# A two-layer hybrid encoder in split fp32: order of matmuls in both linear routines, one PSUM bank for the layer norm's two sums, and the loads and stores at both ends

## The chip, the cores and the metric

The kernel runs on one core of a Trainium2 chip, in one launch. The metric is the device time of that launch in microseconds (us); lower is better. The engines are TensorE (PE in the profile, with its weight loads as PEld), VectorE (DVE), ScalarE (ACT), GpSimd (POOL) and SyncE (SP), which issues most of the DMAs. Each engine works through its own instructions in the order in which they were put there.

## The reference

Two encoder layers on 256 tokens of width 2048, all in float32, with 256 memory tokens:

- layer 0's mixer: RMS norm, then one input projection. Part of its columns go through a gated depthwise convolution of width 31, a layer norm over 1024 channels and a swish; the other part is differential attention with 8 heads. Both results side by side go through one output projection.
- layer 1's mixer: RMS norm, an S5 state-space layer, gelu and a gated projection.
- in both layers, then: cross-attention (4 heads) into the memory tokens, and a gated feed-forward part with a convolution of width 3 and 5632 hidden channels.
- a last RMS norm.

```python
def layer_norm(x, g, b, eps=LN_EPS):
    mu = jnp.mean(xf, axis=-1, keepdims=True)
    var = jnp.mean(jnp.square(xf - mu), axis=-1, keepdims=True)
    y = (xf - mu) * lax.rsqrt(var + eps) * g.astype(jnp.float32) + b.astype(jnp.float32)
...
def mixer_conv_diff(xn, w_in, ...):
    z = xn @ w_in
    a_out = conformer_conv(a_val, a_gate, conv_dw, conv_db, conv_ln_g, conv_ln_b)
    b_out = diff_attention(...)
    return jnp.concatenate([a_out, b_out], axis=-1) @ w_out
```

## The kernel before, in words

**Weights and numbers.** Nearly all of the work is products of activations with large weight matrices. To keep float32 accuracy each operand is split into a high part, rounded to fp32r, and the low rest: a product is high times high, high times low and low times high. `wtile` (L200 to L213) brings in one weight tile of 128x1024 numbers (512 KB): a DMA on SP's queue into `raw` (four buffers, shared with the attention's `kvraw`), a cast on ACT into `hi`, a subtraction on DVE into `lo` (three buffers each).

**lin_ws** (L237 to L256) holds weights stationary. For each of the 16 slices of 128 input channels (kk within a tile, four tiles) and each of two column halves c it issues two matmuls: `both` (L250, weights `hi`, moving the 512 columns [high x, low x]) and a low one (L253, weights `lo`, moving the 256 columns of high x). Both accumulate in the PSUM bank of c: the low one in that bank's half for index 1, since `ps[:, c, 1]` collects all corrections. Low and high alternate, except at the very start of a call. Its users are the input projection (without its value columns), the memory keys, the queries and the feed-forward's up projection.

**lin_xs** (L263 to L291) holds x stationary and moves 512 weight columns: three matmuls (high-high, high-low, low-high) for token block tb = 0 into one bank, then three for tb = 1 into the other. With `tail=3` the last three weight tiles' matmuls for tb = 1 are issued after all those of tb = 0 (L290), which only the very last call uses.

**What sets the order.** Instructions of all engines are put in order by a scheduler that works on the program with a model of times. Side work (the convolution and layer norm `conv_ln`, the S5 parameters) are generators that `background` (L215) advances by a few DVE operations per weight tile, against a credit.

**PSUM.** `pst` (L73) gives single banks under two tags, "ps" and "pt", two buffers each, in turn if no tag is named. The differential attention's heads take "ps" for their scores and "pt" three times each (`ps_wT`, `ps_o`, `ps_oT`). A bank is reused when the reader of the tile that had it two requests earlier under that tag is done. The heads stand ahead of the memory keys and values (`mem_kv`) in the program, and the layer norm's end is played during those, so its two banks `ps_mu` (L516) and `ps_var` (L525) are requested after those of all heads. From `ps_var` come the variance and the reciprocal root on DVE (L528, then `rsqrt_steps`, L109), a multiplication (L532), swish on ACT (L537) and the split into `ao` (L299, L300). `ao` is the second half of the output projection's input (L494 to L500; its first half is the attention's `bo`).

**Start and end.** `setup` (L79) loads the first quarter of x, the identity matrix and the gains on SP, and `mixer0` loads five small tables on POOL's queue (L355 to L363). `xt_first` (L190) loads the other quarters between the first weight tiles, and `transpose_chunk` (L146) transposes them on PE. At the end (L692 to L709) the last quarter of x gets its product added, both token blocks' sums of squares are finished, a Newton iteration gives the reciprocal roots, ACT and DVE scale x, and eight DMAs store it.

## Time and profile before

| | |
|---|---|
| median of 3 runs | 2935.66 us (2931.55 to 2938.13) |
| the profiled execution | 2932.71 us, its span 2930.9 us |
| busy: PE / DVE / ACT / POOL | 98% / 76% / 51% / 9% of the span |
| matmuls | 16769, as many weight loads |
| DMA | 674 MB, 230 GB/s on average |
| granted TensorE clock | 0.994 on average |

The profile is of one execution. Times in its rows count from the first instruction; "[2.35 <-DMA raw]" says that the engine had stood idle for 2.35 us and what ended that. A matmul's own duration holds its way through the array, so two successive matmuls overlap: what one costs in a stream is read from the difference of starts. In rows with "x2" two equal instructions in succession are merged, and the time given is from the first's start to the last's end.

### The profile page before, as it was taken

The page shows a single profiled execution, that of the slowest core. Times are in us where ns is not written, and L with a number is a line of the kernel's source. Part 1 is how long each engine was busy: PE and PEld are TensorE (multiplying, and loading weights), DVE is VectorE, ACT ScalarE, POOL GpSimd, SP SyncE. Part 2 cuts the span into 40 slices and gives each one's busy share as a digit, 9 for nine tenths or more (in the row PEclk, how much of TensorE's full clock was granted, in tenths as well). Part 3 has the DMA queues.
Part 4 walks back from the last instruction along what each step waited for, and adds up shares of the span by engine and source line. Part 5 has one row for each costly group of instructions (what it writes and reads, how often), then busy time and mean ns, then how long its engine had stood idle before and what let it go on. Part 6 is the DMA issues. An engine that isn't in the chain of part 4 may idle for free. (4 is left out here: it accounts for less than half of the span.)

```text
span 2930.9 us, 44468 instructions
## 1 busy us (share of the span) xinstructions
PE 2881.2 (98%) x16769; PEld 2436.5 (83%) x16769; DVE 2213.4 (76%) x3568; ACT 1493.2 (51%) x2015; POOL 268.2 (9%) x509
## 2 busy tenths in 40 slices
PE   8999998999999999999999999999999999999998
PEld 7887887788888888888887787888888888888886
DVE  7899987877899987889855894656567776467764
ACT  5545554554455543455544554545455554345543
POOL 2100022222210012020021121000000000000000
PEclk9999999999999999999999999999999999999999
DMA  6655578988997687776697787655455555555554
GB/s 220 231 188 172 190 238 270 297 260 277 292 297 250 233 272 256 266 254 234 235 316 275 288 328 276 208 187 187 161 191 191 186 188 192 194 189 184 190 188 150
DMA packets 206023, 674.16 MB, mean 230 GB/s; under 512 B 33152, under 2 KB 35728, under 8 KB 205296
## 3 DMA queue, kind: packets, MB, share of 16 engines
q1 hardware_dynamic: 177376, 593.96, 59.1%
q0 software_dynamic: 28432, 77.36, 8.1%
q8 instruction: 131, 2.15, 0.3%
q14 instruction: 84, 0.69, 0.1%
HBM read 620.48 MB, written 61.08 MB: 233 GB/s over the span
## 5 line engine op out<-in xcount | busy, mean ns | idle before, releaser
L211 DVE TENSOR_TENSOR lo<-raw,hi 128x1024 fp32r<-128x1024 f32 x960 | 1173.6, 1224 | 546.1 <-ACT hi L209 542.6
L250 PE MATMUL ps_ws<-x,hi 128*128 128x512 f32 x4352 | 1527.8, 397 | 5.3 <-ACT hi L209 4.4
L209 ACT CAST hi<-raw 128x1024 fp32r<-128x1024 f32 x960 | 1009.0, 1051 | 1005.1 <-PE ps_xs L287 460.8
L253 PE MATMUL ps_ws<-x,lo 128*128 128x256 f32 x4352 | 1202.8, 282 | 2.9 <-DVE lo L211 2.9
L250 PEld LDWEIGHTS ps_ws<-x,hi 128*128 128x128 f32 x4352 | 809.5, 188 | 187.4 <-ACT hi L209 5.2
L253 PEld LDWEIGHTS ps_ws<-x,lo 128*128 128x128 f32 x4352 | 821.6, 189 | 20.0 <-DVE lo L211 5.0
L287 PE MATMUL ps_xs<-hi,hb 128*128 128x512 f32 x1396 | 432.0, 390 | 0.0
L287 PEld LDWEIGHTS ps_xs<-hi,hb 128*128 128x128 f32 x1396 | 262.0, 188 | 53.9
L287 PE MATMUL ps_xs<-lo,hb 128*128 128x512 f32 x698 | 272.3, 390 | 0.0
L287 PE MATMUL ps_xs<-hi,x 128*128 128x512 f32 x640 | 202.8, 395 | 0.2 <-ACT hi L209 0.2
L851 POOL DMA_DIRECT2D w1s<-d_pw x256 | 122.5, 486 | 602.2 <-PE ps_s L438 263.3
L287 PE MATMUL ps_xs<-hi,oT 128*128 128x512 f32 x512 | 160.8, 392 | 0.8 <-ACT hi L209 0.8
L287 PE MATMUL ps_xs<-hi,gT 128*128 128x512 f32 x512 | 159.3, 391 | 0.3 <-ACT hi L209 0.3
L287 PEld LDWEIGHTS ps_xs<-lo,hb 128*128 128x128 f32 x698 | 131.0, 188 | 27.0
L287 PEld LDWEIGHTS ps_xs<-hi,x 128*128 128x128 f32 x640 | 119.9, 189 | 30.3 <-issue 6.1
L287 PE MATMUL ps_xs<-lo,x 128*128 128x512 f32 x320 | 127.3, 398 | 0.0
L259 ACT COPY z<-ps_ws 128x512 f32<-128x512 f32 x88 | 51.7, 587 | 137.6 <-PE ps_ws L250 137.5
L287 PEld LDWEIGHTS ps_xs<-hi,gT 128*128 128x128 f32 x512 | 96.1, 188 | 21.3 <-issue 1.0
L656 ACT ACTIVATE c<-z,fdb,fdw 128x256 f32<-128x256 f32 x176 | 96.2, 595 | 33.0 <-DVE z L651 32.9
L287 PEld LDWEIGHTS ps_xs<-hi,oT 128*128 128x128 f32 x512 | 96.0, 188 | 20.3 <-ACT hi L209 1.0
L512 DVE SCALAR_TENSOR_TENSOR av<-hpt,cdw,av 128x256 f32<-128x256 f32 x240 | 110.7, 485 | 0.7
L260 DVE TENSOR_TENSOR z<-ps_ws,z 128x512 f32<-128x512 f32 x88 | 60.8, 691 | 55.5 <-ACT z L259 55.5
(285 smaller groups left out, 2654.6 us busy)
## 6 DMA issues: line engine op xcount, KB each, us to landing
raw<-ffn_w_up SPq DMA_DIRECT2D x352, 512.0 KB, 3.4
raw<-ffn_w_down SPq DMA_DIRECT2D x176, 512.0 KB, 4.3
raw<-ab_w_in SPq DMA_DIRECT2D x64, 512.0 KB, 3.3
raw<-xa_wv SPq DMA_DIRECT2D x64, 512.0 KB, 3.4
raw<-xa_wk SPq DMA_DIRECT2D x64, 512.0 KB, 4.5
raw<-xa_wq SPq DMA_DIRECT2D x64, 512.0 KB, 4.3
raw<-xa_wo SPq DMA_DIRECT2D x64, 512.0 KB, 3.6
w1s<-d_pw POOLq DMA_DIRECT2D x256, 64.0 KB, 6.1
```

The lines of the kernel that those rows point to most:

```text
L209: nc.scalar.copy(hi, raw)
L211: ins = nc.vector.tensor_tensor(lo, raw, hi.bitcast(F32), op=ALU.subtract)
L250: both = lambda: nc.tensor.matmul(ps[:, c], lhsT=hi[:, kk, sl], rhs=x2, start=first, stop=last)
L253: nc.tensor.matmul(ps[:, c, 1], lhsT=lo[:, kk, sl], rhs=xh, start=False, stop=False)
L259: self.nc.scalar.copy(out, ps[:, :, 1])
L260: self.nc.vector.tensor_tensor(out, ps[:, :, 0], out, op=ALU.add)
L287: ins = mm()
L512: nc.vector.scalar_tensor_tensor(ac[:, ct, :], hp[:, ct, j : j + NTOK], cdw[:, ct, j : j + 1], ac[:, ct, :], op0=ALU.mult, op1=ALU.add)
L656: nc.scalar.activation(c[:, i], zt[:, i, 1 : NTOK + 1], AF.Identity, bias=fdb[:, ft : ft + 1], scale=w(1))
L851: nc.gpsimd.dma_start(pw[t * 16 : t * 16 + 16], self.d_pw[t, k * 4 : k * 4 + 4].partition_broadcast(16))
```

## The change

- In `lin_ws` the two column halves' matmuls of one kind stand together, and slices with odd kk begin with the low ones: high, high, then four low, four high and so on. In `lin_xs` the two token blocks are the inner loop, so that successive matmuls write different banks.
- The layer norm's two sums lie in the two halves of one bank, `ps_ln`, requested once.
- Start: the identity is loaded ahead of x, the very first weight tile through ACT's queue, and the five small tables on SP's queue after the first four weight tiles; what is computed of them follows the gated projection.
- End: the two token blocks of the last product have a bank tile each (`ps_e0`, `ps_e1`), the last quarter's gain is multiplied together with the root, and of the other three quarters ACT scales two and DVE one.
- The Newton iteration takes three DVE operations a round (two where the row is one number wide) where it took four, after one more ahead of it.

The diff, cut to its core:

```diff
@@ setup
+        nc.sync.dma_start(self.ident, a["ident"])
         nc.sync.dma_start(self.X[:, :, 0:512], a["x"][0])
-        nc.sync.dma_start(self.ident, a["ident"])
+        self.begun = False
@@ rsqrt_steps
+        nc.vector.tensor_scalar(v, v, -0.5, None, op0=ALU.mult)
         for it in range(3):
-            nc.vector.tensor_tensor(t, y, y, op=ALU.mult)
-            nc.vector.tensor_tensor(t, t, v, op=ALU.mult)
-            nc.vector.tensor_scalar(t, t, -0.5, 1.5, op0=ALU.mult, op1=ALU.add)
-            nc.vector.tensor_tensor(out if it == 2 else y, y, t, op=ALU.mult)
+            if v.shape[-1] == 1:
+                nc.vector.scalar_tensor_tensor(t, y, y, v, op0=ALU.mult, op1=ALU.mult)
+            else:
+                nc.vector.tensor_tensor(t, y, y, op=ALU.mult)
+                nc.vector.tensor_tensor(t, t, v, op=ALU.mult)
+            nc.vector.scalar_tensor_tensor(out if it == 2 else y, t, 1.5, y, op0=ALU.add, op1=ALU.mult)
@@ wtile
-        dma = nc.sync.dma_start(raw, src)
+        dma = (nc.sync if self.begun else nc.scalar).dma_start(raw, src)
+        self.begun = True
@@ lin_ws
-                for c in range(2):
-                    sl = slice(c * 128, c * 128 + 128)
-                    both = lambda: nc.tensor.matmul(ps[:, c], lhsT=hi[:, kk, sl], rhs=x2, start=first, stop=last)
-                    if first:
-                        both()
-                    nc.tensor.matmul(ps[:, c, 1], lhsT=lo[:, kk, sl], rhs=xh, start=False, stop=False)
-                    if not first:
-                        both()
+                sl = [slice(c * 128, c * 128 + 128) for c in range(2)]
+                both = lambda c: nc.tensor.matmul(ps[:, c], lhsT=hi[:, kk, sl[c]], rhs=x2, start=first, stop=last)
+                low = lambda c: nc.tensor.matmul(ps[:, c, 1], lhsT=lo[:, kk, sl[c]], rhs=xh, start=False, stop=False)
+                for part in (low, both) if kk % 2 else (both, low):
+                    for c in range(2):
+                        part(c)
@@ lin_xs
-                for tb in range(2):
-                    sl = slice(tb * 128, tb * 128 + 128)
-                    ops = [(xh, hi, first, False), (xh, lo, False, False), (xl, hi, False, last)]
-                    for x, y, st, sp in ops:
+                for x, y, st, sp in [(xh, hi, first, False), (xh, lo, False, False), (xl, hi, False, last)]:
+                    for tb in range(2):
+                        sl = slice(tb * 128, tb * 128 + 128)
@@ mixer0
-        nc.gpsimd.dma_start(cdw, a["conv_dw"])
...
                 pv = self.lin_ws(w[n], self.xt_first)
+                for t, v in ((cdw, a["conv_dw"]), (cv, a["conv_v"]), (lq, a["diff_l"].partition_broadcast(128)), (nabs, a["nabs"]), (sub_g, a["subln_g"])):
+                    nc.sync.dma_start(t, v)
@@ conv_ln
-        pm = self.pst("ps_mu")
+        pm = self.pst("ps_ln")
+        pv = pm[:, NTOK:]
+        pm = pm[:, :NTOK]
...
-        pm = self.pst("ps_var")
         for ct in range(8):
-            nc.tensor.matmul(pm[:, :NTOK], lhsT=self.ones, rhs=sq[:, ct, :], start=ct == 0, stop=ct == 7)
+            nc.tensor.matmul(pv, lhsT=self.ones, rhs=sq[:, ct, :], start=ct == 0, stop=ct == 7)
@@ ffn
-                ps = self.lin_xs(a[f"ffn_w_down{layer}"][n, k0 : k0 + nk // KD], hv, list(range(nk)), tail=3 if last and n == 3 else 0)
+                ps = self.lin_xs(a[f"ffn_w_down{layer}"][n, k0 : k0 + nk // KD], hv, list(range(nk)), ps=[self.pst(f"ps_e{tb}", ("ps", "pt")[tb]) for tb in range(2)] if last and n == 3 else None, start=True, tail=3 if last and n == 3 else 0)
...
-            nc.vector.tensor_tensor(x, x, fg[:, 1536:2048], op=ALU.mult)
...
-                if n % 2:
+                if n == 3:
+                    nc.vector.scalar_tensor_tensor(x, x, r, fg[:, 1536:2048], op0=ALU.mult, op1=ALU.mult)
+                elif n:
                     nc.scalar.activation(x, x, AF.Copy, scale=r)
```

How the order of instructions moves is shown at three places.

First, PE's row during the key projection of the memory, before and then now. `lo` and `hi` are weight tiles, `x_2419` and the like the buffers of the transposed memory tokens.

```order
L253 MATMUL ps_ws<-x_2419,lo 128x256
L250 MATMUL ps_ws<-x_2419,hi 128x512
L253 MATMUL ps_ws<-x_2442,lo 128x256
L250 MATMUL ps_ws<-x_2442,hi 128x512
L253 MATMUL ps_ws<-x_2442,lo 128x256
L250 MATMUL ps_ws<-x_2442,hi 128x512
```

```order
L254 MATMUL ps_ws<-x_2394,hi 128x512 x2
L255 MATMUL ps_ws<-x_2394,lo 128x256 x4
L254 MATMUL ps_ws<-x_2394,hi 128x512 x4
L255 MATMUL ps_ws<-x_2394,lo 128x256 x4
L254 MATMUL ps_ws<-x_2394,hi 128x512 x2
L254 MATMUL ps_ws<-x_2417,hi 128x512 x2
```

A tile's 16 matmuls were eight alternations; they are now two high, four low, four high, four low and two high, and the last two run together with the next tile's first two. Where a tile began with a matmul that needs `lo`, it now begins with two that need only `hi`.

Second, PE around the layer norm's second sum (L527, both times), before and then now. `ps_oT` (L476, now L475) is the last step on PE of a head of the differential attention: before it is the eighth head's, now the sixth's.

```order
L287 MATMUL ps_xs<-lo,bo 128x512
L287 MATMUL ps_xs<-hi,bo 128x512 x2
L476 MATMUL ps_oT<-ident,on 128x128 x2
L527 MATMUL ps_var<-sq,ones 128x256 x8
L287 MATMUL ps_xs<-lo,bo 128x512
L287 MATMUL ps_xs<-hi,bo 128x512 x2
```

```order
L254 MATMUL ps_ws<-x_2440,hi 128x512 x2
L527 MATMUL ps_ln<-sq,ones 128x256 x8
L255 MATMUL ps_ws<-x_2440,lo 128x256
L475 MATMUL ps_oT<-ident,on 128x128 x2
L456 MATMUL ps_wT<-ident,s 128x128 x4
```

The sum stood in the output projection, after the last head; it now stands in the key projection, with some 17 weight tiles of it still to come. On DVE the splits that finish `ao` (L300, now L302) stand 18 weight tiles ahead of the first tile that is multiplied with `ao`; before they stood behind that tile and two more.

Third, DVE's last rows, from the last product on, before (down to the first round of the iteration) and then now (without the second block's iteration, which is as the first's).

```order
L694 TENSOR_TENSOR X<-X,ps_xs 128x512 x2
L697 TENSOR_TENSOR X<-X,fg 128x512
L700 TENSOR_REDUCE fv<-ss 128x1
L697 TENSOR_TENSOR X<-X,fg 128x512
L700 TENSOR_REDUCE fv<-ss 128x1
L701 TENSOR_SCALAR fv<-fv 128x1 x2
L111 TENSOR_SCALAR rsq_i<-fv 128x1 x2
L112 TENSOR_SCALAR rsq_i<-rsq_i 128x1 x2
L115 TENSOR_TENSOR rsq_t<-rsq_i 128x1 x2
```

```order
L694 TENSOR_TENSOR X<-X,ps_e_26660 128x512
L699 TENSOR_REDUCE fv<-ss 128x1
L700 TENSOR_SCALAR fv<-fv 128x1
L112 TENSOR_SCALAR rsq_i<-fv 128x1
L113 TENSOR_SCALAR rsq_i<-rsq_i 128x1
...
L122 SCALAR_TENSOR_TENSOR fr<-rsq_t,rsq_i 128x1
L694 TENSOR_TENSOR X<-X,ps_e_26661 128x512
L709 TENSOR_SCALAR X<-X,fr 128x512
L705 SCALAR_TENSOR_TENSOR X<-X,fr,fg 128x512
L699 TENSOR_REDUCE fv<-ss 128x1
```

The two blocks' chains ran side by side; now the first block's whole chain stands ahead of the second block's addition.

More of the change, by code (lines that the diff above doesn't have):

```diff
@@ L261, in add_parts, with lin_xs @@
         return out
-    def lin_xs(self, w, xt, kts, ps=None, stop=True, tail=0):
+    def lin_xs(self, w, xt, kts, ps=None, stop=True, tail=0, start=False):
         nc = self.nc
-        start = ps is None
-        if start:
+        start = start or ps is None
+        if ps is None:
             ps = self.acc.tile([128, 2, 512], F32, tag="acc", name="ps_xs")
```

26 lines of the change are left out of this document (11 added, 15 removed).

## The prediction

> **What bounds the kernel now.** I read the page first: the busy times and PE's 40 slices.
>
> ```profile
> PE 2881.2 (98%) x16769; PEld 2436.5 (83%) x16769; DVE 2213.4 (76%) x3568; ACT 1493.2 (51%) x2015; POOL 268.2 (9%) x509
> ...
> PE   8999998999999999999999999999999999999998
> ```
>
> PE is the bound in every slice but three: the first, the seventh (440 to 513 us) and the last. So time is won in two ways: by what one matmul costs in the stream, and by the waits in those three places. Next I asked for busy time by stage, whose columns are the stretch, its length, the busy time of PE, PEld, DVE, ACT and POOL with instructions, and then the granted clock, the DMA share and GB/s.
>
> ```profile
> 453.00:480.00 27.00, 26.06 (x118) 21.05 (x118) 24.03 (x49) 10.81 (x18) 7.72 (x16) 1.00 0.97 317
> 480.00:545.00 65.00, 51.10 (x209) 40.45 (x208) 49.94 (x68) 34.22 (x50) 11.45 (x24) 0.87 0.78 250
> ```
>
> The output projection (453 to 545 us) loses 14 us of PE in its second part, at a clock of 0.87. The list of waits says for what PE waited there.
>
> ```profile
> PE ps_xs L287 <- ACT ao L299: 9.9, 1, 9.9
> PE ps_xs L287 <- DVE lo L211: 5.4, 9, 1.5
> ...
> PE ps_ws L253 <- DVE lo L211: 2.9, 4, 2.0
> ```
>
> One wait of 9.9 us is for `ao`, the layer norm's result. The tiles of its two sums show why that is late.
>
> ```profile
> L518 PE MATMUL ps_mu<-av,ones x16: 379/379/382, 397.6 to 400.8; 128*128 128x256 f32 x16
> ...
> L527 PE MATMUL ps_var<-sq,ones x16: 379/379/382, 471.1 to 474.3; 128*128 128x256 f32 x16
> ```
>
> The first sum ends at 401, the second starts 70 us later, though only two subtractions and two squares lie between: its bank was held by the attention's heads.
>
> **The change: the stationary weights.** The count and the recorded load time come from the groups by line:
>
> ```profile
> L211 DVE TENSOR_TENSOR lo<-raw,hi 128x1024 fp32r<-128x1024 f32 x960 | 1173.6, 1224 | 546.1 <-ACT hi L209 542.6
> L250 PE MATMUL ps_ws<-x,hi 128*128 128x512 f32 x4352 | 1527.8, 397 | 5.3 <-ACT hi L209 4.4
> ...
> L253 PEld LDWEIGHTS ps_ws<-x,lo 128*128 128x128 f32 x4352 | 821.6, 189 | 20.0 <-DVE lo L211 5.0
> ```
>
> There are 4352 pairs of a high and a low matmul, eight to a weight tile, so 544 of the 960 tiles; the other 416 are `lin_xs`'s, with 12 matmuls each (4992). What a pair costs is read in a stage that holds little else, the view by stage for L250 alone (length, PE, PEld, clock, DMA share, GB/s):
>
> ```profile
> 2200.00:2450.00 250.00, 248.33 (x710) 131.71 (x710) 1.00 0.55 188
> ```
>
> 250 us for 710 pairs: 352 ns (the stage's few other matmuls are in it). The new order has two equal neighbours where there was always one of each. The old order shows that only where one call follows another, in PE's timeline:
>
> ```profile
> 440.46 0.28 PE L253 MATMUL ps_ws<-x,lo 128*128 128x256 f32 x1
> 440.57 0.40 PE L250 MATMUL ps_ws<-x,hi 128*128 128x512 f32 x1
> 440.81 0.28 PE L253 MATMUL ps_ws<-x,lo 128*128 128x256 f32 x1
> ...
> 440.94 0.62 PE L250 MATMUL ps_ws<-x,hi 128*128 128x512 f32 x2
> 441.40 0.28 PE L253 MATMUL ps_ws<-x,lo 128*128 128x256 f32 x1
> ...
> 441.74 0.40 PE L253 MATMUL ps_ws<-x,lo 128*128 128x256 f32 x2
> 441.98 0.40 PE L250 MATMUL ps_ws<-x,hi 128*128 128x512 f32 x1
> ```
>
> By starts, a pair takes 0.35 us, two highs 0.46 (230 ns each), two lows 0.24 (120 each). Longer runs exist elsewhere: 512 columns with a new load each in `lin_xs`, 256 columns with a new load each in the cross-attention's products (first and last of nine).
>
> ```profile
> 694.13 0.61 PE L287 MATMUL ps_xs<-hi,oT 128*128 128x512 f32 x2
> ...
> 694.81 0.61 PE L287 MATMUL ps_xs<-hi,oT 128*128 128x512 f32 x2
> ```
>
> ```profile
> 2032.97 0.28 PE L576 MATMUL ps_xs<-kT,qT 128*128 128x256 f32 x1
> ...
> 2033.92 0.28 PE L575 MATMUL ps_xs<-kT,qT 128*128 128x256 f32 x1
> ```
>
> Three steps in 0.68 us are 227 ns; eight in 0.95 are 119. So a pair in runs costs between 230 + 120 = 350 and 227 + 119 = 346 ns. In a run of four the first still follows the other kind, so I count three of four at the new price: 0.75 x 4352 x 2 to 6 ns = 6.5 to 20 us. I take **11 us**, nearer the small end, because those rows are of this routine's own instructions; for the range 0 to 20, zero because 2 ns is within what starts rounded to 10 ns can show.
>
> In `lin_xs` the banks now change at every matmul. The old order changes banks at every third, and the 0.68 us above hold three steps with such a change at an even 227: **0**, and 2 us either way for the range (4992 matmuls by 0.4 ns, what rounding of the starts leaves open).
>
> Both routines now need `lo` two high matmuls after a tile's start rather than at once or one later. The 13 waits for `lo` above can shrink by at most 0.23 us (`lin_xs`) or 0.46 (`lin_ws`) each, 9 x 0.23 + 4 x 0.46 = 3.9 us in all; several are shorter or due to loads: **1 us**.
>
> **The layer norm's bank.** With both sums in one bank the second no longer waits for a head. The order puts `ao`'s end 18 weight tiles ahead of its reader; at 8 pairs of 352 ns a tile that is 50 us of cover, so the 9.9 us go entirely. What is late next are weight tiles: the DMA share was 0.97 just ahead of the stall, and the stall itself let loads catch up. PE stayed 26.06 of 27 us busy at that share, so I give back only **2 us** (0 to 6). There is also the clock:
>
> ```profile
> 481.00:491.20 10.20, 0.32 (x2) 0.00 (x0) 8.10 (x12) 5.39 (x9) 0.00 (x0) 0.65 0.85 285
> 491.20:494.30 3.10, 3.04 (x7) 2.42 (x8) 1.75 (x3) 3.04 (x7) 0.00 (x0) 0.50 0.02 5
> ...
> 531.00:539.00 8.00, 6.47 (x17) 5.07 (x17) 6.72 (x10) 3.34 (x4) 3.09 (x7) 0.57 0.89 309
> ```
>
> After the stall PE worked 3.1 us at half clock, which is **1.5 us** lost that goes too. The Trainium skill (TensorE: Matmul & The Clock Gate, "Part 1: The HAM clock gate") says that the clock halves after an idle window of some 3.4 us and comes back after a busy one; by it the loss would be an estimated 1.7 us, and the trace agrees. By the same rule the second stretch should not exist, since no wait ahead of it reaches 3.4 us; the trace differs. So that one (8 us at 0.57, 3.4 us lost) may stay or go: I count none of it, and keep it for the range.
>
> The layer norm's own iteration and the heads' get shorter by DVE operations of 0.16 to 0.43 us; with the stall gone nothing on PE waits for them: 0.
>
> **The end.**
>
> ```profile
> 2915.89 0.39 PE L290 MATMUL ps_xs<-hi,hb 128*128 128x512 f32 x1
> 2916.32 1.29 DVE L694 TENSOR_TENSOR X<-X,ps_xs 128x512 f32<-128x512 f32 x2 [5.85 <-PE ps_xs L290]
> 2917.04 0.63 ACT L696 ACTIVATE junk<-X 128x512 f32<-128x512 f32 x1 [7.83 <-DVE X L694]
> ...
> 2919.16 0.15 DVE L700 TENSOR_REDUCE fv<-ss 128x1 f32<-128x4 f32 x1
> ...
> 2922.09 2.56 ACT L706 ACTIVATE X<-X,fr 128x512 f32<-128x512 f32 x4 [3.57 <-DVE fr L118]
> ...
> 2922.61 4.47 SPq L709 DMA_DIRECT2D out<-X  x8
> ```
>
> The last matmul ends at 2916.28, the span at 2930.9: a tail of 14.6 us. Both additions waited for the last matmul, though the first block's were done 18 matmuls (18 x 227 ns = 4.1 us) earlier. With two tiles the first block's chain and its four stores run under those. Left for the second block: addition 0.65, square 0.8, eleven dependent DVE steps (16 took 2.9 us: 0.19 each, so 2.1), 0.5 to the first store, four issues of 0.56 (4.47 / 8) = 2.2, and 3.8 from the last issue's end (2927.08) to the span's end: 10.1. The first block's scalings stand between on DVE and ACT, some 0.4. So 14.6 - 10.5 = **4.1 us** (3 to 4.5).
>
> **The start.**
>
> ```profile
> 0.74 0.66 SPq L83 DMA_DIRECT2D X<-x  x1
> ...
> 2.55 0.43 SPq L204 DMA_DIRECT2D raw<-ab_w_in  x1
> ...
> 4.55 0.63 ACT L128 ACTIVATE junk<-X 128x512 f32<-128x512 f32 x1 [2.53 <-DMA X<-x]
> ...
> 10.02 1.04 ACT L209 CAST hi<-raw 128x1024 fp32r<-128x1024 f32 x1 [2.35 <-DMA raw<-ab_w_in]
> ...
> 12.92 0.63 ACT L128 ACTIVATE junk<-X 128x512 f32<-128x512 f32 x1 [1.12 <-DMA X<-x]
> ```
>
> The first tile's load took from 2.55 to 10.02 us, behind three others; x took from 0.74 to 4.55. Issued first on ACT's queue it lands as x did or as late as now, 4.6 to 8 us. But ACT works through four chunks of casts and sums without pause:
>
> ```profile
> 16.40:26.40 10.00, 9.12 (x58) 7.93 (x58) 9.12 (x29) 9.99 (x25) 0.00 (x0) 1.00 0.69 256
> ```
>
> so at most its idle 2.35 + 1.12 = 3.5 us are won. Against it: the cast now stands ahead of the sums on ACT, PE transposes x's second quarter ahead of the first product, and the tables come later on SP, behind which the fifth weight tile queues; two of ACT's operations on them (L431, now L430) stand ahead of the last quarter's casts. I take **1 us** (-1.5 to 3). POOL's queue only loses work.
>
> **Sum.** 11 + 0 + 1 + 9.9 - 2 + 1.5 + 4.1 + 1 = 26.5 us. The profiled execution took 2932.7 (span 2930.9), so 2906.2; the median of the three runs is 3.0 above it, which gives **2909** for the comparison.
>
> **Rivals.**
> - *Runs do nothing*: the 2 ns are rounding, and the pair stays at 352. Then 15.5 us remain: 2935.7 - 15.5 = 2920. For it: the single pairs' rows are that close. Chance 0.25.
> - *Runs reach the long runs' prices throughout*: 20 instead of 11, so 2900. For it: 227 and 119 are steady rows with a load for each matmul. Chance 0.15.
> - *Loads take the stall's place*: the stall shrinks to a chain of shorter waits for weight tiles, and of 9.9 us only some 3 are won: 2909 + 5 = 2914; with the clock's second stretch growing by one such 2916. For it: 0.97 of DMA just ahead; against it: 0.78 in the stage as a whole. Chance 0.12.
> - *Slower: lows in runs are held by their loads*. A load is recorded at 189 ns, longer than a low matmul's step of 119; alternating, every low's load lay under a high matmul. If three of four lows took 189, that is 0.75 x 4352 x 70 ns = 228 us: 2920 + 228 = 3148. It decides from the point where a run's low costs 15.5 us / 3264 = 5 ns more than alternating with nothing gained on the highs. Against it: the product's nine matmuls above, each with a load of its own, at 119. Chance 0.03. The Trainium skill (the same page, "LDWEIGHTS (loading the stationary operand)") gives columns / 1.2 GHz, an estimated 107 ns for these 128 columns: by it loads just fit under lows with nothing to spare, the slower case has no price, and the trace, at 119, agrees.
>
> **How the numbers follow.** The forecast has 0.45 and the four rivals 0.55. All but one are faster. The best ends together (runs 20, loads 0, clock 3.4 more, end 4.5, start 3, `lo` 3.9) are 46 us: 2890; the worst (runs 0, loads 6, clock 0, end 3, start -1.5, `lo` 0) win 5: 2930. Neither will come all together, so the range is **2892 to 2924**. A difference of 0.2%, 6 us, is about what a measurement of this kernel can tell from none. Faster by more 0.93, within it 0.04, slower 0.03.
>
> **What would show it.** In the new profile: L254's count by stage at 348 to 350 ns a pair; starts in a run of lows 117 to 120 apart; no wait of PE for `ao`, the second sum within some 10 us of the first; PE's idle time between 440 and 545 down by about 8 us; the tail after the last matmul near 10.5 us; the first high product ahead of 11 us. I would be wrong if a run's lows stood over 125 ns apart, if waits for `hi` or `lo` in the output projection added up to over 8 us, or if a stage without any of these edges' waits (the S5 part) got longer through the scheduler's new order.

## The result, and the profile after

The changed kernel takes 2918.5 us in the median of 4 runs (2915.7 to 2919.5), the kernel before on the same chip 2934.5 us in 4 (2931.6 to 2938.1): a ratio of 0.994, with a 95% interval of 0.993 to 0.996. That is faster, by 16 us and inside the range, but 9.5 us above the forecast 2909 and next to the rival "runs do nothing" (2920). The profiled execution took 2919.5 us, its span is 2917.7: 13.2 us less than before, where the sum said 26.5.

The page of the changed kernel, busy times and PE's slices: the dip in the seventh slice is gone, and PE is busy 4.5 us less.

```profile
PE 2876.7 (99%) x16769; PEld 2434.8 (83%) x16769; DVE 2204.0 (76%) x3524; ACT 1492.2 (51%) x2015; POOL 266.4 (9%) x504
...
PE   8999999999999999999999999999999999999998
```

**Where the time went.** Three rows by tile give marks along the program: the first copy of the gate's sums (end of the start), the first and the last product of the two cross-attentions' outputs (`oT`: after layer 0's output projection and queries, and ahead of layer 1's feed-forward part), and the last high matmul of `lin_ws`. The columns are shortest, median and longest time, and first and last start. First the kernel before, then the changed one:

```profile
L259 ACT COPY sg<-ps_ws x4: 567/588/591, 41.3 to 111.2; 128x512 f32<-128x512 f32 x4
L287 PE MATMUL ps_xs<-hi,oT x512: 387/389/502, 679.9 to 2178.6; 128*128 128x512 f32 x171
L250 PE MATMUL ps_ws<-x,hi x4352: 387/395/793, 11.1 to 2807.1; 128*128 128x512 f32 x198
```

```profile
L262 ACT COPY sg<-ps_ws x4: 567/586/587, 37.7 to 108.4; 128x512 f32<-128x512 f32 x4
L289 PE MATMUL ps_xs<-hi,oT x512: 387/389/497, 673.3 to 2172.1; 128*128 128x512 f32 x171
L254 PE MATMUL ps_ws<-x,hi x4352: 387/396/776, 10.5 to 2797.9; 128*128 128x512 f32 x198
```

| mark | before | after | difference | won since the mark above |
|---|---|---|---|---|
| first `sg` | 41.3 | 37.7 | -3.6 | 3.6 (start) |
| first `oT` | 679.9 | 673.3 | -6.6 | 3.0 (layer norm, its loads, the clock) |
| last `oT` | 2178.6 | 2172.1 | -6.5 | -0.1 |
| last high | 2807.1 | 2797.9 | -9.2 | 2.7 (layer 1's feed-forward part) |
| end of span | 2930.9 | 2917.7 | -13.2 | 4.0 (tail) |

So the start and the tail gave 7.6 us together, the layer norm 3.0 and the runs 2.7, where the sum had 5.1, 9.4 (9.9 - 2 + 1.5) and 11, and 1 more for `lo`.

**The layer norm.** Both sums now stand together, 7.5 us from the last start of the first to the first start of the second:

```profile
L519 PE MATMUL ps_ln<-av,ones x16: 378/379/382, 386.1 to 390.2; 128*128 128x256 f32 x16
...
L527 PE MATMUL ps_ln<-sq,ones x16: 377/379/379, 397.7 to 400.9; 128*128 128x256 f32 x16
```

PE no longer waits for `ao`, and in the two stretches that the prediction watched it works 26.30 + 59.60 us of 92, where it worked 26.06 + 51.10 (stretch, length, busy time of the engines, clock, DMA share, GB/s):

```profile
453.00:480.00 27.00, 26.30 (x119) 20.76 (x120) 22.69 (x41) 10.57 (x13) 8.95 (x19) 1.00 0.93 314
480.00:545.00 65.00, 59.60 (x261) 47.14 (x261) 50.76 (x64) 32.89 (x47) 17.86 (x38) 0.97 0.95 300
```

That is 8.7 us less idle time, as forecast. But the waits only moved out of those stretches. In the memory keys ahead of them and in the queries behind them PE now idles 1.85 and 2.83 us. The kernel before, then the changed one:

```profile
400.00:450.00 50.00, 50.00 (x292) 43.75 (x291) 44.65 (x87) 22.42 (x32) 13.68 (x29) 1.00 0.77 255
550.00:650.00 100.00, 99.69 (x586) 87.54 (x585) 81.69 (x126) 52.82 (x76) 24.25 (x51) 1.00 0.85 271
```

```profile
400.00:450.00 50.00, 48.15 (x281) 41.54 (x281) 41.58 (x74) 27.80 (x45) 11.50 (x24) 1.00 0.73 225
550.00:650.00 100.00, 97.17 (x579) 85.10 (x578) 81.33 (x123) 50.48 (x69) 23.00 (x48) 1.00 0.86 271
```

PE's largest waits from 400 to 660 us in the changed kernel (total, times, longest), all for weight tiles and their splits:

```profile
PE ps_ws L255 <- DVE lo L216: 3.7, 5, 1.3
PE ps_xs L289 <- ACT hi L214: 3.1, 3, 1.8
PE ps_xs L289 <- DVE lo L216: 2.8, 5, 0.7
```

**The clock.** Of the two stretches at half clock the first went, and of the second (531.8 to 538.6 us before, 6.8 us, PE busy for 6.05 of them) 3.4 us are left:

```profile
518.00:523.00 5.00, 2.95 (x12) 1.80 (x10) 3.86 (x6) 2.20 (x3) 0.00 (x0) 1.00 1.02 369
523.60:527.00 3.40, 3.11 (x8) 1.97 (x7) 3.18 (x5) 2.12 (x4) 0.00 (x0) 0.50 0.76 236
```

**The runs.** Three runs of four highs and four lows in PE's timeline, from the same stage as the prediction's 352 ns:

```profile
2310.64 1.09 PE L254 MATMUL ps_ws<-x,hi 128*128 128x512 f32 x4
2311.57 0.63 PE L255 MATMUL ps_ws<-x,lo 128*128 128x256 f32 x4
2312.04 1.09 PE L254 MATMUL ps_ws<-x,hi 128*128 128x512 f32 x4
...
2314.85 1.09 PE L254 MATMUL ps_ws<-x,hi 128*128 128x512 f32 x4
```

2314.85 - 2310.64 = 4.21 us for 12 pairs: 351 ns, of it 0.93 us for four highs (232 each) and 0.47 for four lows (118 each). The forecast's 11 us are 2.5 ns for each of the 4352 pairs: 349.5 where it had 352.

**The two ends.** The last matmul starts at 2906.72 and ends at 2907.11; from there to the end of the span are 10.6 us (forecast 10.5, before 14.6). One block's addition and square are left, and the first block's scaling already runs:

```profile
2906.72 1.34 ACT L707 ACTIVATE X<-X,fr 128x512 f32<-128x512 f32 x2 [2.20 <-DVE fr L122]
2906.72 0.39 PE L292 MATMUL ps_e<-hi,hb 128*128 128x512 f32 x1
2907.15 0.69 DVE L694 TENSOR_TENSOR X<-X,ps_e 128x512 f32<-128x512 f32 x1 [0.46 <-PE ps_e L292]
2907.47 5.82 SPq L710 DMA_DIRECT2D out<-X  x8
```

At the start the first tile is cast at 4.78 us instead of 10.02, the first transposes start 1.5 us later than before (6.69 against 5.22), and the first high product stands at 10.46 (before 11.1):

```profile
4.78 1.04 ACT L214 CAST hi<-raw 128x1024 fp32r<-128x1024 f32 x1 [2.32 <-DMA raw<-ab_w_in]
...
6.69 1.94 PE L160 MATMUL ps_xt<-ident,X 128*128 128x128 f32 x8 [6.69 <-DMA X<-x]
...
10.46 1.20 PE L254 MATMUL ps_ws<-x,hi 128*128 128x512 f32 x2
```

### The profile page after: what moved, and what is told of

The parts are those of the page before. It is cut to its first block, busy times and chain, and to the rows that moved or that the text cites. A ratio compares the mean times of both kernels' runs of the same rounds, so it can differ in the third digit from the quotient of the medians.

```text
span 2917.7 us, 44422 instructions
## 1 busy us (share of the span) xinstructions
PE 2876.7 (99%) x16769; PEld 2434.8 (83%) x16769; DVE 2204.0 (76%) x3524; ACT 1492.2 (51%) x2015; POOL 266.4 (9%) x504
## 5 line engine op out<-in xcount | busy, mean ns | idle before, releaser
L254 PE MATMUL ps_ws<-x,hi 128*128 128x512 f32 x4352 | 1199.4, 395 | 5.3 <-ACT hi L214 2.9
L254 PEld LDWEIGHTS ps_ws<-x,hi 128*128 128x128 f32 x4352 | 742.7, 189 | 105.6 <-ACT hi L214 4.9
L255 PEld LDWEIGHTS ps_ws<-x,lo 128*128 128x128 f32 x4352 | 665.9, 189 | 97.6 <-DVE lo L216 6.8
L255 PE MATMUL ps_ws<-x,lo 128*128 128x256 f32 x4352 | 701.4, 282 | 3.9 <-DVE lo L216 3.9
L289 PE MATMUL ps_xs<-hi,hb 128*128 128x512 f32 x1328 | 357.7, 390 | 0.0
L289 PE MATMUL ps_xs<-lo,hb 128*128 128x512 f32 x664 | 205.0, 390 | 0.0
L289 PE MATMUL ps_xs<-hi,x 128*128 128x512 f32 x640 | 178.3, 395 | 1.2 <-ACT hi L214 1.2
L289 PE MATMUL ps_xs<-hi,oT 128*128 128x512 f32 x512 | 141.1, 392 | 0.8 <-ACT hi L214 0.8
L289 PE MATMUL ps_xs<-hi,gT 128*128 128x512 f32 x512 | 139.1, 391 | 0.5 <-ACT hi L214 0.5
L289 PEld LDWEIGHTS ps_xs<-hi,gT 128*128 128x128 f32 x512 | 95.6, 188 | 21.8 <-ACT hi L214 1.2
L289 PEld LDWEIGHTS ps_xs<-hi,oT 128*128 128x128 f32 x512 | 95.3, 188 | 20.1 <-ACT hi L214 1.0
L289 PE MATMUL ps_xs<-lo,x 128*128 128x512 f32 x320 | 101.4, 396 | 0.0
```

Source lines behind the costliest of these rows:

```text
L254: both = lambda c: nc.tensor.matmul(ps[:, c], lhsT=hi[:, kk, sl[c]], rhs=x2, start=first, stop=last)
L255: low = lambda c: nc.tensor.matmul(ps[:, c, 1], lhsT=lo[:, kk, sl[c]], rhs=xh, start=False, stop=False)
L289: ins = mm()
```

## The experiments

Each kernel was timed beside the kernel before. "Steps of the stream" in the expectations are the distances between successive starts on PE, as far as they are more than 25 ns over the median of their kind (line and width), added up by stretches of 50 us: from 400 to 650 us 23.6 us before and 20.1 in the changed kernel. Matmuls at half clock have longer steps too, so these sums hold that loss as well.

### The runs: alone (e1), and all else without them (e2)

```diff
-                for c in range(2):
-                    sl = slice(c * 128, c * 128 + 128)
-                    both = lambda: ...
...
+                for part in (low, both) if kk % 2 else (both, low):
+                    for c in range(2):
+                        part(c)
```

e1 is the kernel before with this hunk, e2 the changed kernel without it.

> The kernel before with the new order of the stationary-weight matmuls alone (four high, four low). Theory A, from the starts in the changed kernel's trace: only the third and fourth high of a run get cheaper, the lows get 1.6 ns dearer, and a pair wins 0.6 ns. 4352 pairs: 2.5 us less time, 0.1%, not to be told from none by the time; the pair by starts 350 to 351 ns. Rival B, the forecast's price: 11 us less (348.5 ns a pair), and the 13 us that the changed kernel falls short of it were lost elsewhere. Rival C: the runs also let the waits for the low halves grow or shrink, by 1 to 4 us, which the waits of PE for lo would show.

> The changed kernel with the old alternation of high and low matmuls put back, all else new. Theory A: 2.5 us slower than the changed kernel, so some 13 us faster than the kernel before. Rival B: 11 us slower than the changed kernel, so some 5 us faster than the kernel before. Theory A and e1 should agree: the runs' share taken away and added alone are the same.

e1: 2933.7 us against 2932.3, ratio 1.0002 (0.9993 to 1.0012). e2: 2921.8 us against the same, 0.996 (0.9947 to 0.9973), which is 3.2 us above the changed kernel by the medians and 5 by the two ratios. So the runs are worth nothing that the time shows when alone, and some 3 to 5 us beside the rest. Rival B's 11 us is excluded by e1; the times of e2 and of the changed kernel alone would just leave room for it, their marks do not. The marks of e1, then of e2:

```profile
L285 PE MATMUL ps_xs<-hi,oT x512: 387/389/502, 682.2 to 2182.3; 128*128 128x512 f32 x171
L249 PE MATMUL ps_ws<-x,hi x4352: 387/396/796, 11.5 to 2808.2; 128*128 128x512 f32 x198
```

```profile
L291 PE MATMUL ps_xs<-hi,oT x512: 387/389/497, 674.0 to 2172.5; 128*128 128x512 f32 x171
L255 PE MATMUL ps_ws<-x,hi x4352: 387/396/775, 10.5 to 2800.9; 128*128 128x512 f32 x198
```

From the last `oT` to the last high lie layer 1's 1408 pairs. That takes 628.5 us before (2807.1 - 2178.6), 628.4 in e2, 625.9 in e1 and 625.8 in the changed kernel: the runs win 2.6 us there, 1.9 ns a pair, whatever else is changed. The other 2944 pairs show no such gain. The mean price of a pair by stage, from starts whose neighbours both belong to the stream and without steps held by a wait (ns; high plus low):

```
us from the start   20-215  345-440  570-660  740-870  870-1040  1190-1400  2200-2450
before              350.8   349.4    349.8    349.6    349.0     350.4      352.7
e2, alternating     350.1   350.8    351.5    350.1    350.1     350.4      352.5
after, four         350.4   350.6    350.2    350.3    350.2     350.5      350.8
e7, eight           349.2   348.8    349.5    348.7    348.7     349.2      349.2
```

The alternating order costs 352.7 only in layer 1's feed-forward part (352.5 in e2), and 349.0 to 351.5 elsewhere. The prediction read its 352 in exactly that stage (2200 to 2450) and put it on all 4352 pairs. In runs of four a high costs 232 ns in every stage, alternating 232.7 to 234.5 and in layer 1's feed-forward part 235.6; but a low costs 118.4 in runs and 116.7 alternating, which outside layer 1 takes the gain back. And by place in a run of four the highs step 234.1, 234.1, 231.5 and 228.5 ns: it is not three of four that cost 227, only the last is near it. Of C the waits for `lo` came, and shrank: with the runs alone from 8.3 to 6.0 us in all; but PE's waits for `hi` grew from 6.9 to 13.3, though in one profiled execution only.

### The layer norm's bank alone (e3)

```diff
-        pm = self.pst("ps_mu")
+        pm = self.pst("ps_ln")
+        pv = pm[:, NTOK:]
+        pm = pm[:, :NTOK]
```

> The kernel before with both sums of the layer norm in one bank, nothing else. The wait of 9.9 us for the layer norm's result goes in every theory. Theory D: the loads and the vector engine's splits give some 5 to 7 us of it back as a chain of waits of 0.5 to 2 us for weight tiles in the key projection and the output projection (400 to 650 us), so 3 to 6 us less time (the half clock after the stall, 1.5 us, included). Rival E, the forecast: 2 us given back and 1.5 us of clock won, so 9.4 us less time.

2931.6 us, ratio 0.9996 (0.9988 to 1.0005): even less than theory D's 3 to 6, and the forecast's 9.4 is excluded. The wait for `ao` is gone, yet at the first `oT` only 1.4 us of it are left (678.5 against 679.9), and SP's queue shows a suspect (queue, line, what its next instruction waited for; total, times, longest, from 400 to 650 us):

```profile
L287 PE MATMUL ps_xs<-hi,oT x512: 387/389/502, 678.5 to 2178.7; 128*128 128x512 f32 x171
```

```profile
SPq L853 <- DMA d_w<-w1s: 63.7, 15, 9.2
```

L853 loads `s5_b1` into a buffer of the S5 side work (`s5_w1`: per step 0.5 MB of `d_pw` on POOL's queue, 0.5 MB of `s5_b1` and a store of 0.5 MB on SP's). It has to wait until the store of the step before last has landed, and the weight tiles' loads stand behind it on the same queue. But the kernel before has the same wait at this load:

```profile
SPq L852 <- DMA d_w<-w1s: 57.3, 15, 7.5
```

So it is not new, and what it costs needs a run (e9). The clock gave something back as well: in e3's execution PE stood at half clock from 510.3 to 513.8, 527.4 to 534.2 and 626.4 to 629.8 us, busy for 12.8 us of it, which costs up to 6.4 us; before, the two stretches cost up to 4.5.

### The end alone (e4)

The diff of `ffn` and of the last loop, with the `start` argument of `lin_xs`.

> The kernel before with the end's edits alone (a bank of its own for each token block of the last product, the last scaling fused, three of four scalings changed in place). The forecast: the tail after the last matmul goes from 14.6 us to some 10.5 us and the time falls by 4.1 us. Rival: the two banks taken from the rings of the small products make the last product wait, and less than 3 us is won.

2930.6 us, ratio 0.9991 (0.9981 to 1.0001), so 2.6 us less, and 0 to 6 by the interval. Its last matmul ends at 2916.1 and its span at 2927.9: a tail of 11.8 us, 2.8 less than before and 1.2 more than in the changed kernel. The rival's reason is not seen, since the last matmul is no later than before. What lacks is the shorter Newton iteration, which was left out of this kernel: the first block's steps still run on DVE when the second block's addition is due, and the second block's iteration has 14 steps:

```profile
2916.12 0.69 DVE L694 TENSOR_TENSOR X<-X,ps_e 128x512 f32<-128x512 f32 x1 [0.53 <-PE ps_e L290]
...
2918.98 0.15 DVE L111 TENSOR_SCALAR rsq_i<-fv 128x1 int32<-128x1 int32 x1
...
2921.47 0.16 DVE L118 TENSOR_TENSOR fr<-rsq_i,rsq_t 128x1 f32<-128x1 f32 x1
```

From 2918.98 to 2921.67, when ACT can scale, are 2.7 us; the changed kernel's nine steps take 1.8 (2909.18 to 2910.97 in its timeline). That is 0.9 of the 1.2 us; the rest fits the first block's later steps. So the end's gain is 2.8 us for the banks and scalings, and, by difference, some 1.2 for the iteration.

### The start alone (e5), and its first tile alone (e6)

```diff
-        dma = nc.sync.dma_start(raw, src)
+        dma = (nc.sync if self.begun else nc.scalar).dma_start(raw, src)
+        self.begun = True
```

e5 has all the start's edits (ident ahead of x, tables later, `lam` later); e6 only these lines.

> The kernel before with the start's edits alone (ident ahead of x, the first weight tile on ACT's queue, the five tables later and on SP's). Theory F, from the traces: the 64th matmul of the stationary-weight stream starts 3.5 us earlier in the changed kernel and in the kernel with all but the runs, and stays so until the layer norm; so the start alone is worth 3 to 4 us. Rival, the forecast: 1 us.

> The kernel before with one edit: the first weight tile's load is issued on ACT's queue. Theory F1: the early tile does the start's work, 3 to 4 us as in the kernel with all the start's edits. Rival F2: the tables' five transfers, which in this kernel still stand on POOL's queue at the start, are what delayed the tile; then less than 1 us is won here and the rest only with all the edits.

e5: 2930.3 us, ratio 0.9991 (0.9983 to 1.0). e6: 2930.8, 0.9993 (0.9985 to 1.0002). The times don't tell them apart, the marks do (e5, then e6; before 41.3):

```profile
L261 ACT COPY sg<-ps_ws x4: 566/587/587, 37.6 to 109.6; 128x512 f32<-128x512 f32 x4
```

```profile
L261 ACT COPY sg<-ps_ws x4: 567/586/587, 40.9 to 112.6; 128x512 f32<-128x512 f32 x4
```

All the start's edits win 3.7 us by then, the early tile alone 0.4, and even that is no more than executions differ by: e4, e9 and e12, whose start is as before, have this mark at 40.5, 40.9 and 41.5. So F2 was right that the tile alone wins under 1 us. But what comes late with the five tables at the start is x's second quarter (in e6 ACT and PE wait over 3 us for it at 11.7; in the changed kernel it is there at 8.9). So the other edits win some 3 us, the tables' place most likely the larger part; the identity's and `lam`'s new places were not run apart from it. In e5's profiled execution only 1.0 us of it were left at the last `oT` (2177.6 against 2178.6); the S5 part between varies by 2 to 3 us among these kernels without a cause that was found.

### Runs of eight (e7)

```diff
-                for part in (low, both) if kk % 2 else (both, low):
-                    for c in range(2):
-                        part(c)
+                ops[0].append(both)
+                ops[1].append(low)
+            if k4 == 3:
+                ops[1].append(ops[0].pop())
+            for part in ops[0] + ops[1]:
+                for c in range(2):
+                    part(c)
```

In a call's last tile the last slice's two highs come after the lows, which closes the sums.

> The changed kernel with runs of eight: all eight high matmuls of a weight tile, then its eight lows. In runs of four the highs step 234, 234, 231.5 and 228.5 ns. Theory G: a run has a price of entry, and the highs from the third on go at some 227 to 228 ns; then a pair takes 348 ns and 9 to 11 us are won on the changed kernel. Rival H: the mean of 232 ns is what a high of this routine costs wherever it stands (its moving operand is the pair of token halves, not one row as in lin_xs); then a pair stays at 350 to 351 ns and the time is the changed kernel's within 3 us. In both, the low halves are needed eight matmuls later, so PE's waits for lo (8.5 us in the changed kernel) shrink to less than half.

2900.1 us (2898.5 to 2901.3), ratio 0.9885 (0.9871 to 0.9898): 18.5 us under the changed kernel and more than either theory said. In PE's timeline two full rounds of eight lows and eight highs take 2321.15 - 2315.56 = 5.59 us, 349 ns a pair:

```profile
2315.56 2.00 PE L255 MATMUL ps_ws<-x,hi 128*128 128x512 f32 x8
2317.40 1.11 PE L256 MATMUL ps_ws<-x,lo 128*128 128x256 f32 x8
...
2321.15 1.55 PE L255 MATMUL ps_ws<-x,hi 128*128 128x512 f32 x6
```

That is between G (348) and H (350 to 351). The highs of the middle of a run step 229 ns on average, the last 227, the first two 233 and 236; the lows 119. The marks:

```profile
L294 PE MATMUL ps_xs<-hi,oT x512: 387/389/499, 665.3 to 2154.8; 128*128 128x512 f32 x171
L255 PE MATMUL ps_ws<-x,hi x4352: 387/393/775, 10.6 to 2778.3; 128*128 128x512 f32 x198
```

Layer 1's feed-forward part takes 623.5 us, 2.3 less than with runs of four: 1.6 ns a pair; by the table it is 0.7 to 1.8 in the other stages, so some 6 us for all 4352. The other 13 or so of the 19.6 us that e7's last high is ahead of the changed kernel's are waits and clock (the stretch at half clock in S5 is 3.4 us long instead of 6.8). At `lin_ws` the waits for weight tiles are gone: the groups by line show

```profile
L255 PE MATMUL ps_ws<-x,hi 128*128 128x512 f32 x4352 | 1104.9, 394 | 1.5 <-DVE x L168 1.4
...
L256 PE MATMUL ps_ws<-x,lo 128*128 128x256 f32 x4352 | 612.7, 283 | 0.0
```

where the changed kernel has 5.3 us ahead of highs and 3.9 ahead of lows:

```profile
L254 PE MATMUL ps_ws<-x,hi 128*128 128x512 f32 x4352 | 1199.4, 395 | 5.3 <-ACT hi L214 2.9 <-DVE x L168 2.3
...
L255 PE MATMUL ps_ws<-x,lo 128*128 128x256 f32 x4352 | 701.4, 282 | 3.9 <-DVE lo L216 3.9
```

The low halves are needed eight highs (1.8 us) after the high ones instead of two, which covers DVE's 1.22 us for the split. That this is why the waits went is argued, not shown; and at `lin_xs` those for `lo` stay (5.1 us, 4.6 in the changed kernel), so that all waits for `lo` fall from 8.5 to 5.1 us, not to less than half. Some 6 us of the gain fall between the first and the last `oT` beyond the price of the pairs there; which waits made them was not taken apart.

### The side work held back (e8)

```diff
-... "kv": 0.95, "out": 0.8, "wq": .7, ...
+... "kv": 0.55, "out": 0.4, "wq": .8, ...
```

> The changed kernel with three numbers of the planner changed: the background work for S5 goes slower while the key and value memory and the output projection run (rates 0.55 and 0.4 instead of 0.95 and 0.8) and a little faster in the cross-attention's queries (0.8 instead of 0.7). Theory D: that work's transfers (1.5 MB a step) and its vector operations are what the weight tiles wait for after the stall is gone, so PE's waits between 400 and 650 us (20 us in the changed kernel by the steps of the stream) fall to less than half and the time falls by 5 to 10 us. Rival: the weight tiles of these products alone fill the transfer engines, and the waits stay within 4 us of what they were. Risk: work that ends too late for S5 shows as a wait before 1560 us.

2923.9 us, ratio 0.996 (0.9947 to 0.9974): 5 us slower than the changed kernel by the medians, though the two intervals overlap. The waits from 400 to 650 us fell from 20.1 to 15.8 us by the steps, not to half, and the first `oT` came at 667.4, 5.9 us earlier than in the changed kernel. But the layer norm is played from the same queue of side work and came late again (PE waits 3.8 us for `ao`), and the held-back steps now ran into the feed-forward part, where PE waits for `hi`:

```profile
PE ps_ws L254 <- ACT hi L214: 5.0, 4, 2.0
```

(790 to 900 us; the changed kernel waits 0.7 us there.) At the last `oT` it is 4.7 us late (2176.8 against 2172.1). The relief shows in this execution, and was given back later.

### The load that waits, on another queue (e9, e10), and lo last in lin_xs too (e11)

```diff
-            nc.sync.dma_start(b.rearrange("p g c d -> p (g c d)"), a["s5_b1"][k])
+            nc.gpsimd.dma_start(b.rearrange("p g c d -> p (g c d)"), a["s5_b1"][k])
```

e9 is e3 with this line, e10 is e7 with it. e11 is e10 with, per weight tile of `lin_xs`, the eight matmuls with `hi` ahead of the four with `lo`.

> The kernel with the layer norm's bank alone (e3), and one line more: the background work's load of s5_b1 is issued on POOL's queue instead of SP's. In e3 SP's queue stood 64 us between 400 and 650 us at that load (15 times, up to 9.2 us), which waits for the store before it to land, and the weight tiles' loads queue behind it. Theory D2: that order, not the amount of data, gave the bank's gain back; then PE's waits for hi and lo between 500 and 650 us, 17 us in e3 by the steps of the stream, fall under 6 us, and the time is 7 to 12 us under the kernel before. Rival D1: the transfer engines are full (0.9 of their time in this stage) whatever the queue; then the waits stay over 12 us and the time is that of e3, within 3 us of the kernel before.

> Runs of eight (e7) with the same load on POOL's queue. By theory D2 the waits that e7 still has between 500 and 650 us (13 us by the steps of the stream) fall to some 5 us: 2892 us, 8 us under e7. By rival D1 the time is e7's, 2900 us.

> As e10, and in lin_xs the eight products with the high part of a weight tile stand ahead of the four with its low part, so that lo is needed 8 matmuls (1.8 us) after hi and not 2. If what the runs of eight won beside their price was time for lo, the same must show here: PE's waits for lo at lin_xs (5.1 us in e7) fall under 1.5 us and the time by some 3 us against e10. If those waits are late loads, hi waits in lo's place and the time stays within 1 us of e10.

e9: 2927.0 us, ratio 0.9974 (0.9962 to 0.9985). One line about a queue turns the bank's gain of 0.04% of the time into 0.26%, some 7.6 us. The waits from 500 to 650 us fell from 16.9 to 7.6 us by the steps (D2 said under 6), those from 450 to 500 rose from 2.8 to 6.6, and the first `oT` stands at 672.7, 5.8 us ahead of e3:

```profile
L287 PE MATMUL ps_xs<-hi,oT x512: 387/389/502, 672.7 to 2173.1; 128*128 128x512 f32 x171
```

By the time D2 is the better theory, but its reason is not shown, since the two executions differ in the granted clock (the number ahead of the DMA share; e3, then e9):

```profile
500.00:650.00 150.00, 141.78 (x748) 120.77 (x747) 119.21 (x174) 75.14 (x105) 34.38 (x72) 0.95 0.86 281
```

```profile
500.00:650.00 150.00, 145.21 (x801) 124.28 (x800) 124.58 (x181) 78.09 (x111) 40.06 (x83) 1.00 0.88 289
```

From 400 to 650 us the steps hold 22.3 us in e3, some 6 of them at half clock, and 16.9 in e9, 1.7 of them at half clock (479.3 to 482.7 us). What is left are some 16 and 15 us: most of the 5.8 us is clock and not shorter waits. The other runs agree as far as their mean clock tells: 0.995 or 0.996 in e3's, 0.996 to 0.998 in e9's, whose two fastest (2919.7 and 2922.4 us) have the highest. Nor does SP's queue wait less in e9: it waits 140.7 us for `lo` ahead of the weight tiles' loads, 95.6 in e3. What the line wins with the old bank was not run.

e10: 2897.9 us (2896.2 to 2901.3), not to be told from e7's 2900.1, its first `oT` at 666.1 against 665.3: here D1 had the time right. From 500 to 650 us the steps hold 12.9 us in e7 and 11.4 in e10, where D2 said some 5. Ahead of that, in e7

```profile
450.00:500.00 50.00, 50.00 (x232) 41.56 (x232) 43.11 (x66) 23.05 (x31) 19.08 (x40) 1.00 0.99 335
```

PE works without a gap at a DMA share of 0.99, so nothing is left to win in these 50 us. That the transfers set the pace behind them, at a share of 0.88, is D1's reason and not shown.

e11: 2899.0 us, not to be told from e10. PE no longer waits for `lo` anywhere in `lin_xs` (6.1 us in e10); some other waits grew, to 3.5 us for `tq` in S5 (1.7 in e10) and 1.0 for an attention head, but those for `hi` at `lin_xs` did not (2.6, 3.7 in e10). Both ratios are 0.988, each known to some 4 us, so the 3 us of the first theory are neither seen nor excluded.

### The side work's data (e12)

```diff
-            for t in range(8):
+            for t in range(8 if k < 2 else 0):
```

> As e9 (the bank alone, s5_b1 on POOL's queue), and the background work leaves out a third of its data: the eight loads of 64 KB of d_pw for each step but the first two, 0.5 of 1.5 MB a step (the vector operations and their pace stay; S5's tables come out of old data). It tells apart what is left of the waits between 450 and 650 us in e9, 14 us by the steps of the stream. Theory D1': what is left is the amount of data; then these waits fall under 8 us and the 2000th low matmul of the stationary-weight stream, 6.9 us ahead of the kernel before in e9, comes 11 us or more ahead. Rival: what is left is the vector engine's splits, or the weight tiles' own loads; then the waits stay at 12 to 15 us.

(The mark in it is the 2000th matmul of the stationary-weight stream, highs and lows counted.) 2919.3 us, ratio 0.9955 (0.9941 to 0.9969). The mark comes 11.8 us ahead of the kernel before, the waits from 450 to 650 us fall from 14.3 to 8.7 us by the steps, a little over the 8 expected, and the first `oT` is 12.2 us early. From 450 to 600 us, e9 and then e12:

```profile
450.00:600.00 150.00, 141.07 (x697) 117.15 (x696) 121.71 (x193) 72.01 (x104) 43.90 (x90) 0.99 0.90 295
```

```profile
450.00:600.00 150.00, 145.25 (x732) 121.08 (x731) 127.56 (x201) 76.05 (x109) 5.28 (x10) 1.00 0.77 267
```

The DMA share falls from 0.90 to 0.77 and PE works 4.2 us more, with DVE busier than before: its splits were not the limit. So with one bank, one queue and a third of the side data away, the first `oT` is 12 us earlier; in e3 it was 1.4. In e12's execution no stretch between the start and S5 is at half clock, which is part of that. What the lighter side work would win with the old bank was not run, so the 12 us are those of the three together.

## Why the prediction was right, and where not

- **The answer** (faster by more than 0.2%, 2892 to 2924) held. The end was well sized, the start too small by 2.6 us, and the two largest terms, 11 and 9.4, measured 2.7 and 3.0. That the time fell next to the first rival's 2920 is chance: the rival keeps the 9.4 and takes 5.1 for the two ends, which gave 7.6. The range held because it took the runs down to 0 and had room for loads in the stall's place.
- **The runs, 11 us: the step "count 4352 at a price read in one stage" failed**, in two ways. The old order's 352 ns is layer 1's feed-forward part alone; elsewhere it cost 349 to 351 (table above). And for the new order it took three highs of four near the long run's price of 227 to 230 ns; they came to 232 on average, and two of four stay at 234. What the rows of the trace could have told: the same quotient in a second stage. The rival "runs do nothing" had the size nearly right, by the wrong reason: they win 1.9 ns a pair in a third of the places.
- **`lo`, 1 us: nothing.** PE's waits for it were 8.3 us and are 8.5, those for `hi` went from 6.9 to 8.6. Needing `lo` only two highs into a tile did not shorten them.
- **The layer norm: the mechanism was right, the bill was not.** The wait for `ao` went entirely, the idle time between 440 and 545 us fell by the 8 us named as a sign. The term "2 us given back to loads" is what failed: with the bank alone (e3) all but 1.4 us came back, as shorter waits, in part outside the stretch that was watched, and as time at half clock. This was the rival "loads take the stall's place", at a price larger than its own (it left 3 us). Its evidence stood in the prediction: a DMA share of 0.97 just ahead of the stall. The argument against it, 0.78 in the stage as a whole, averaged over the stall itself, in which loads caught up. What e9 and e12 add is that most of it can be had, with one load on another queue and a third of the side work's data left out. How much of that is waits and how much clock stays open, and so does what either edit wins with the old bank.
- **The clock, 1.5 us**: the first stretch went, and the second shrank, which had been left out of the sum. The prediction's 3.4 us for the second took all of its 8 us as work; half of what PE was busy at half clock is 3.0. So the gain is 1.5 + 3.0 - 1.6 = 2.9 us. It lies in the 3.0 of the marks, so the waits of that stage gave about nothing net. Nor does the clock follow from the bank: with the bank alone (e3) the half clock came three times.
- **The end, 4.1 us**: 4.0 in the profile. Right, with a tail of 10.6 against 10.5; its eleven steps had the shorter iteration in them, which by e4 is worth some 1.2.
- **The start, 1 us**: 3.6, above its range. The bound by ACT's idle time, 3.5, was reached; what failed is the 2.5 us taken off it. What the forecast put at nothing ("POOL's queue only loses work") was most likely the larger part: with the tables' loads at the start x's second quarter came 3 us later.
- **`lin_xs`'s change of banks, 0**: right. e2 has it and takes 628.4 us for the stretch with 576 of its matmuls, before 628.5; over the whole program the step is 227.1 ns in both.
- **The slower rival** (lows held by their loads at over 125 ns) did not come: 119 in runs of four, 119 in runs of eight.

## What to carry to other kernels

A price per instruction is to be read in every stage that it will be multiplied over; a stage that "holds little else" is clean, and may be the only one of its kind. When a stall is taken out of a stage whose transfers are nearly full just beside it, count the stall as won only as far as the loads can follow, and look for the new waits on both sides of the place. Before calling a stage limited by bandwidth, look at what stands at the head of the queue that brings its data: here one load, waiting for a store, kept the queue for 64 us in 250, and moving it won some 6 us beside the one bank (e9 against e3). But see whether the wait is new (it was 57 us before the change), and take the time at half clock out before two executions' waits are compared. And an order of matmuls can be worth more by the waits it leaves than by what its neighbours cost: runs of eight won some 13 us by the one and 6 by the other, though why the waits went was not shown.

## What was not expected of the hardware

- The alternating stream of a 512- and a 256-column matmul has no single price: 349.0 to 352.7 ns a pair in the same kernel, steady for hundreds of us in a stage, with highs of 230, 232, 233, 236 and 241 ns as the commonest steps. Runs of four (350.2 to 350.8) and of eight (348.7 to 349.5) vary less. Why was not found.
- A high does not reach its long-run step (227 ns in `lin_xs`) behind one equal neighbour: in runs of eight the first two take 233 and 236, the middle ones 229 on average.
- The granted clock halved in the changed kernel at 523.6 us though no wait of PE ahead of it was longer than 1.8 us; PE had been busy 2.95 of the 5 us before. The Trainium skill (TensorE: Matmul & The Clock Gate, "Part 1: The HAM clock gate") ties the half clock to an idle window of some 3.4 us, and tells of one kernel in which short idles between groups of matmuls brought it. The 3.4 us that it lasted fit that window, and here too a chain of short waits was enough to start it.
- The wait of a load for the landing of a store, up to 9.2 us each in e3, on the queue that the weight tiles' loads share.
